# Heads of a hybrid layer: z units in the attention stage, gate units behind the heads, recurrence steps at every fifth matmul, half-height groups of two heads joined

## The chip, the cores and the metric

The kernel runs on one core of a Trainium2 chip. The metric is the device time of one execution in microseconds (us), as the median of several runs. TensorE (PE, its weight loads PEld) multiplies matrices into PSUM, ScalarE (ACT) and VectorE (DVE) empty PSUM and work on SBUF, GpSimd (POOL) and SyncE (SP) mainly issue transfers here.

## What is computed

One layer of a hybrid decoder trunk on x (1024 tokens x 1024 channels, f32). Its input is modulated by a conditioning vector c, projected by `w_in`, and goes through two mixers side by side, windowed attention and a gated delta rule; sigmoid gates merge them, and a squared-ReLU MLP follows.

```
mod = silu(c) @ w_ada + b_ada
sh1, sc1, gt1, sh2, sc2, gt2 = split(mod, 6)
u = x * (1 + sc1) + sh1
qa, ka, va, dq, dk, dv, z, b_raw, a_raw, g_a, g_b = split(u @ w_in)
y_a = sliding_window_attention(qa, ka, va, sinks) @ w_oa
y_b = gated_deltanet(dq, dk, dv, z, b_raw, a_raw, ...) @ w_ob
mixed = (sigmoid(g_a) * y_a + sigmoid(g_b) * y_b) @ w_out
x = layer_norm(ALPHA * x + (1 + gt1) * mixed)
u2 = x * (1 + sc2) + sh2
x = layer_norm(ALPHA * x + (1 + gt2) * (relu(u2 @ w_ff1 + b_ff1)**2 @ w_ff2 + b_ff2))
```

The gated delta net has 8 heads of width 128. q, k and v go through a causal convolution of four taps and a Silu. Then each head runs a recurrence over the tokens with a state of 128x128, and closes with a norm and a multiplication by silu(z):

```
v_new = u_c - w_c @ state
o_c = q_c @ state + intra_c @ v_new
state = state * last_c + k_c.T @ v_new
o = o * rsqrt(mean(o * o) + RMS_EPS) * norm_w * silu(z)
```

## The kernel before

**The stream of main matmuls.** A projection is made 128 output channels at a time. Such a unit is 48 main matmuls: two halves of 512 tokens, eight blocks of input channels, and for each of these three products of f32 numbers split in a high and a low part (`wh`, `wl` of the weights, `uh`, `ul` of the input). `stream_unit` issues them, all on L253 in this part of the kernel. One main matmul is a moving tile of 128x512 with 128x128 weights. A counter goes up with every main matmul, and all other work is hung on it: `at(i, f)` runs the function f ahead of the i-th main matmul, `after(n, f)` runs it n matmuls from now. This writes the order of the program: each engine works through its own instructions in the order in which the functions issued them, and semaphores do the rest.

**The stages.** k convolutions and v of the attention come first. Then 26 units make the attention stage (`units_b`): 2 of k, 8 of q and 16 gate units, behind which the softmax work of the attention is hidden. The gate units are g_a and g_b; `gate_done` copies both halves of a unit to SBUF and stores them to DRAM. From main matmul Q0 on, 24 units make the heads stage: q, v and z of head 0, of head 1, and so on. Then come `w_oa` (8 units, called ya here), `w_ob` (yb), the output projection and the MLP.

**The heads.** A head's work is small steps among the main matmuls:
- `hd_load` fetches what an earlier stage left in DRAM for the head (`kT`, `kd`, `E`, `Re`, `TT`, `T2o`, and `T1`, `L21`, which are 64 high).
- `conv_done` takes q's and v's projections out of PSUM: ScalarE copies each half to `pad` (L958) and, scaled, to `qT` or `vT` (L959), VectorE adds three taps (L962), ScalarE does a Silu (L967). One half after another, so that a unit's two halves stand 24 matmuls apart.
- `hd_z` (L1064) and `hd_x` (L1074) finish the inverse of a 128x128 triangular block by two groups of eight matmuls of 64x64 with 64-high operands, the half-height groups; ScalarE copies their PSUM tile to `Z` (L1065) and to `TT` (L1079, two copies).
- `hd_kq` (L1103) multiplies k and q in four pairs of blocks, VectorE makes `E` of it (L1107); `hd_qturn` (L1090) and `hd_vturn` (L1121) transpose q and v.
- The recurrence has 8 chunks of three steps. `hd_a`: one matmul kT x St (L1133), then VectorE makes `rhs` (L1135). `hd_b`: one matmul TT x rhs (L1143), then ScalarE makes `vn` (L1145). `hd_c`: the state's update (L1153; VectorE adds it to `St`, L1158) and the output, two matmuls into PSUM tile "c" (L1166), which ScalarE squares (`junk`, L1168) and VectorE copies (`o`, L1169). Chunk 0 has no kT x St, and its `rhs` is a slice of `vr`.
- `hd_norm` (L1174 to L1184) takes one Sqrt on ScalarE (`fs`, L1176) and scales `o`; `hd_out` transposes `o` and multiplies it by `sz`, which GpSimd stores to `og_d`. `sz` is silu(z), made by ScalarE right from z's PSUM tile (`sz_done`, L1206).

**Where the steps stand.** HOP = 6: a step stands at every sixth main matmul, so a chunk takes 18 and a head 144, which are just the three units of a head. Head h's recurrence starts at R = Q0 + 140 + 144h (28 later for head 7, whose recurrence lies in ya). The groups of `hd_z` and `hd_x` stand alone, at Q0 + 144h + 74 and + 86 (for heads past the first).

**PSUM tiles.** mains: "mm". Tag "a" (two buffers): the recurrence's products. Tag "c" (one): its output. Tag "b" (two buffers): kq, z, x, the transposes. A group that asks for a third "b" tile takes the place of the one that is emptied first, and waits for its readers.

**Between them.** `ada_load`, `ada_add` and `ada_part` (L995 to L1023) compute the last four sections of `mod`: VectorE sums 8 weight rows in an accumulator, and PE sums it over partitions, for f below 4 by one matmul of 128x512 (L1009), for the others by four pairs of 128x1 (L1018). ScalarE splits every unit's weights to `wh` (L220), VectorE makes `wl` (L221), both for a whole unit at once.

Of the kernel before, what the change touches and what calls it, by code (L numbers as in the profile page):

```python
# [34 lines left out]
def hybrid_layer_kernel(ctx: ExitStack, tc: tile.TileContext,  # L35
# [112 lines left out]
    wseq = [in_cols(w_in, C_DK + h * P) for h in range(8)]  # L148
    gates = [C_GA + f * P for f in range(KT)] + [C_GB + f * P for f in range(KT)]
    units_b, gi_, qi_, ki_ = [], 0, 0, 0  # L150
    for kind in "gkqgqggqggqkqggqggqggqgggg":
        if kind == "g":
            units_b.append((kind, gi_))
            gi_ += 1
        elif kind == "q":
            units_b.append((kind, qi_))
            qi_ += 1
        else:
            units_b.append((kind, ki_))
# [46 lines left out]
    def after(n, f, *args):  # L206
        at(count[0] + n, f, *args)
# [573 lines left out]
    def gate_done(i):  # L781
        t = gpool.tile([P, S], F32, tag="gate", name="gate")

        def done(half, pt):
            A.activation(out=t[:, halves[half]], in_=pt, func=AF.Copy)
            if half == 1:
                nc.sync.dma_start(out=(ga_d if i < KT else gb_d)[i % KT], in_=t)
        return done
# [197 lines left out]
    def ada_load(i, f, k):  # L986
        w, lo = ada["w"][i % 3], ada_cols_of(f)
        if k < KT:
            nc.sync.dma_start(out=w, in_=w_ada[k * P:(k + 1) * P, lo:lo + HALF])
            after(28, ada_add, w, k)  # L990
        else:
            nc.sync.dma_start(out=w[0:1, :], in_=b_ada[None, lo:lo + HALF])
        if k == KT - 1 + (f < 4):
            after(28 if f < 4 else 35, ada_part, f, w[0:1, :])

# [6 lines left out]

    def ada_part(f, b):
        acc = ada["acc"][:, 0, :]
        lo = ada_cols_of(f)
        half = f % 2
        t = psum("a", 2)
        if f < 4:
            T.matmul(t, lhsT=ones, rhs=acc, start=True, stop=True)  # L1009

            def put():
                V.scalar_tensor_tensor(out=b, in0=t[0:1, :], scalar=1.0, in1=b, op0=ALU.add, op1=ALU.add)
                nc.gpsimd.dma_start(out=gt_d[f // 2:f // 2 + 1, halves[half]], in_=b)
            after(5, put)
            return
        dst = (sh2 if f < 6 else sc2)[:, 4 * half:4 * half + 4]
# [13 lines left out]
    items = [(f, k) for f in range(KT) for k in range(KT + (f < 4))]  # L1030
    at(Q0 + 20, ada_open)
    for i, (f, k) in enumerate(items):
        at(Q0 + 170 + 13 * i, ada_load, i, f, k)

    def hd_load(h):
# [3 lines left out]
        T1 = d["T1"] = big4("T1", shape=[P, 4, 64])  # L1039
        L21 = d["L21"] = big4("L21", shape=[P, 4, 64])  # L1040
        T2o = d["T2o"] = big4("T2o", shape=[64, 4, 64])
# [10 lines left out]
        nc.gpsimd.dma_start(out=d["kd"], in_=kd_d[h])  # L1052
        d["ssq"] = pc.tile([P, NT], F32, tag="ssq", name="ssq")
        d["sso"] = pc.tile([P, NT], F32, tag="sso", name="sso")
        d["vr"], d["o"] = big4("vr"), big4("o")

# [90 lines left out]
    def hd_c(h, n):  # L1147
# [20 lines left out]
        after(4, lambda: A.activation(out=junk(), in_=op_[:, 0:P], func=AF.Square, accum_out=d["sso"][:, n:n + 1]))  # L1168
# [20 lines left out]
    def hd_out(h, half):  # L1189
        d = heads[h]  # L1190
        tp = psum("b", 2)
        for j in range(4):
            T.transpose(tp[:, chunk(j)], d["o"][:, chunk(4 * half + j)], ident)

# [6 lines left out]

    def sz_done(h):
        def done(half, pt):
            if half == 0:
                heads[h]["sz"] = big4("sz")
            A.activation(out=heads[h]["sz"][:, halves[half]], in_=pt, func=AF.Silu)  # L1206
        return done

    HOP = 6
    for h in range(8):  # L1210
        b = Q0 + 144 * h
        at(max(b, OPEN + 1), hd_load, h)
        late = max(b, OPEN + 1)
        for half in range(2):
            at(b + (56 if h else 68) + 24 * half, hd_qturn, h, half)
            at(max(b + 62, late + 40) + 24 * half, hd_kq, h, half)
            at(b + (98 if h else 104) + 24 * half, hd_vturn, h, half)
        at(max(b + 74, late + 50), hd_z, h)
        at(max(b + 86, late + 70), hd_x, h)
        R = b + (140 if h < 7 else 168)  # L1220
# [22 lines left out]

    for h in range(8):
        heads[h]["qT"] = pce.tile([P, S], F32, tag="qT", name="qT", bufs=2)
        stream_unit(uh, ul, conv_done(pce, h, heads[h]["qT"]))
        heads[h]["vT"] = pce.tile([P, S], F32, tag="vT", name="vT")
        stream_unit(uh, ul, conv_done(pce, 16 + h, heads[h]["vT"]))
        if h == 7:
            for k in range(KT):  # L1250
                at(count[0] + (0, 0, 0, 26, 36, 32, 38, 44)[k], attn_load, k)
                at(count[0] + (8, 14, 20, 38, 55, 50, 60, 66)[k], attn_split, k)
        stream_unit(uh, ul, sz_done(h), interleave=h == 7)

# [11 lines left out]

    CLOSE = R + 3 * HOP * NT + 36
    oh, ol = [None] * KT, [None] * KT
# [769 lines left out]
```

## Time and profile before

| what | value |
|---|---|
| median of 3 runs | 1820.82 us (1819.68 to 1826.78) |
| the profiled execution | 1820.36 us, of which its span is 1818.6 |
| mean granted TensorE clock | 0.995 |
| busy: DVE, ACT, POOL | 69%, 56%, 17% of the span |
| heads stage | about 548 to 890 us |
| ya stage, with head 7's recurrence | 890 to 975 us |

One execution was profiled. Times of day in it are us from the start of its span, and a line number is that of the kernel before unless the text says otherwise. A row of an engine's timeline has the start, the duration, the engine, the line, the operation, output <- inputs, weights and moving shape, the count; in brackets stands the idle time ahead of it and what ended it. A row of the windows has the stretch in us, its length, and for PE, its weight loads, DVE, ACT, POOL and SP the busy time and the count of instructions, then the granted clock, the DMA share and the GB/s.

### The profile page before, as it was taken

Reading aid. Unit: us, or ns where it says so; the run is one execution under the profiler, and the core shown is the slowest. Engines: PE = TensorE matmul, PEld = TensorE weight load, DVE = VectorE, ACT = ScalarE, POOL = GpSimd, SP = SyncE. Lnnn points to the kernel's source line nnn. Section 1 sums busy time; section 2 is a strip of 40 time slices with the busy share of each in tenths; the row PEclk is TensorE's granted clock in tenths of the full one; section 3 lists DMA queues with packets and bytes.
Section 4 is the critical chain, followed back from the end, with each engine's and each line's share of the span. In section 5 each row is a group of like instructions: output and inputs, shape, how many; then the busy total and the mean of one; then the engine's idle time right before and its main releaser. Section 6 shows DMA issues by size and latency. Waiting matters only on the chain.

```text
span 1818.6 us, 26129 instructions
## 1 busy us (share of the span) xinstructions
PE 1801.8 (99%) x9161; PEld 1512.8 (83%) x9161; DVE 1260.7 (69%) x2362; ACT 1017.5 (56%) x2304; POOL 304.2 (17%) x458
## 2 busy tenths in 40 slices
PE   8999999999999999999999999999999999999998
PEld 6988888888888888888888888888888888888887
DVE  6688688887854666666654445789777766576697
ACT  4699678888874555555554322466555554434341
POOL 0233234444331000000001100002222220000000
PEclk8999999999999999999999999999999999999999
DMA  9756722232257555554456543459887879755671
GB/s 275 209 199 204 231 68 89 66 104 80 78 194 173 153 147 157 152 154 137 135 176 235 165 149 139 138 157 315 292 295 265 286 281 390 258 185 186 199 264 47
DMA packets 262237, 337.73 MB, mean 186 GB/s; under 512 B 26213, under 2 KB 171318, under 8 KB 261850
## 3 DMA queue, kind: packets, MB, share of 16 engines
q1 hardware_dynamic: 223642, 216.09, 38.1%
q0 software_dynamic: 30320, 103.20, 17.0%
q10 hardware_dynamic: 8144, 16.78, 2.6%
q8 instruction: 72, 1.18, 0.3%
q14 instruction: 59, 0.48, 0.1%
HBM read 231.40 MB, written 102.51 MB: 184 GB/s over the span
## 4 chain that ended last, share of the span: by engine, by line
PE 90%; DVE 3%; ACT 2%; DMA 1%; issue 1%; POOL 0%; ACTq 0%; DVEq 0%; POOLq 0%; SPq 0%
PE mm L253 40%; PE mm L1899 8%; PE mm L1959 7%; PE a L1959 4%; PE b L1899 4%; PE b L1959 4%; PE a L1899 3%; PE c L1959 2%; PE c L883 2%; PE mm L1525 1%; PE mm L191 1%; PE mm L192 1%; PE mm L193 1%; PE a L809 1%; PE a L1525 1%; PE a L808 1%
## 5 line engine op out<-in xcount | busy, mean ns | idle before, releaser
L253 PE MATMUL mm<-uh,wl 128*128 128x512 f32 x800 | 330.1, 413 | 0.0
L253 PE MATMUL mm<-ul,wh 128*128 128x512 f32 x800 | 314.7, 393 | 0.0
L253 PE MATMUL mm<-uh,wh 128*128 128x512 f32 x800 | 313.9, 392 | 0.0
L221 DVE TENSOR_TENSOR sp<-sraw,sp 128x1024 fp32r<-128x1024 f32 x112 | 132.7, 1220 | 75.7 <-ACT sp L220 75.7
L220 ACT ACTIVATE sp<-sraw 128x1024 fp32r<-128x1024 f32 x112 | 112.6, 1054 | 121.4 <-PE b L1959 75.4
L253 PEld LDWEIGHTS mm<-ul,wh 128*128 128x128 f32 x800 | 150.2, 188 | 31.8
L253 PEld LDWEIGHTS mm<-uh,wl 128*128 128x128 f32 x800 | 150.8, 188 | 26.3 <-issue 1.0
L253 PEld LDWEIGHTS mm<-uh,wh 128*128 128x128 f32 x800 | 150.9, 189 | 25.4 <-issue 1.0
L1959 PE MATMUL mm<-sp 128*128 128x512 f32 x528 | 136.0, 389 | 0.0
L1959 PEld LDWEIGHTS mm<-sp 128*128 128x128 f32 x528 | 98.8, 188 | 20.3
L221 DVE TENSOR_TENSOR wl<-wr,wh 128x1024 fp32r<-128x1024 f32 x80 | 98.3, 1228 | 8.4 <-ACT wh L220 6.5
L220 ACT ACTIVATE wh<-wr 128x1024 fp32r<-128x1024 f32 x80 | 83.9, 1049 | 20.6 <-PE c L1525 12.3
L1959 PE MATMUL a<-sp 128*128 128x512 f32 x336 | 92.3, 389 | 0.0
L816 DVE CUSTOM_DVE_ANT_0 nscore<-a,amask,nsink 128x256 f32<-128x256 f32 (+1 forms) x128 | 54.5, 464 | 44.8 <-PE a L809 44.5
L1959 PE MATMUL b<-sp 128*128 128x512 f32 (+1 forms) x336 | 79.7, 374 | 0.0
L1959 PEld LDWEIGHTS a<-sp 128*128 128x128 f32 x336 | 63.1, 188 | 13.1
L1145 ACT ACTIVATE vn<-a,brk 128x128 f32<-128x128 f32 x64 | 23.5, 367 | 89.1 <-PE a L1143 89.0
L1959 PEld LDWEIGHTS b<-sp 128*128 128x128 f32 x336 | 60.3, 188 | 11.2
L827 POOL TENSOR_TENSOR sm<-sm 128x256 f32<-128x256 f32 x56 | 50.9, 909 | 104.9 <-ACT sm L823 76.6
L221 DVE TENSOR_TENSOR wl<-fraw,wh 128x1024 fp32r<-128x1024 f32 x43 | 52.5, 1221 | 19.6 <-ACT wh L220 19.5
L823 ACT ACTIVATE sm<-nscore,stat 128x257 f32<-128x257 f32 (+1 forms) x128 | 62.0, 488 | 2.7 <-DVE stat L816 2.4
L220 ACT ACTIVATE wh<-fraw 128x1024 fp32r<-128x1024 f32 x43 | 44.9, 1055 | 31.0 <-PE b L1899 25.0
(539 smaller groups left out, 4646.6 us busy)
## 6 DMA issues: line engine op xcount, KB each, us to landing
wr<-in_w_in_dram SPq DMA_DIRECT2D x60, 512.0 KB, 3.9
sraw<-hf_d SPq DMA_DIRECT2D x54, 512.0 KB, 4.3
adaw<-in_w_ada_dram SPq DMA_DIRECT2D x73, 256.0 KB, 4.7
fraw<-in_w_ff_dram SPq DMA_DIRECT2D x32, 512.0 KB, 5.3
sraw<-wt_d SPq DMA_DIRECT2D x32, 512.0 KB, 4.5
hf_d<-t ACTq DMA_DIRECT2D x48, 256.0 KB, 3.8
wt_d<-wx POOLq DMA_DIRECT2D x48, 256.0 KB, 3.6
sraw<-in_w_ff_dram SPq DMA_DIRECT2D x22, 512.0 KB, 5.5
```

What stands on the lines that cost most here:

```text
L191: T.matmul(t, lhsT=wh[:, k, :], rhs=xh[k][:, sl], start=k == 0, stop=False)
L220: A.activation(out=hi, in_=src, func=AF.Copy)
L221: after(lag, lambda: V.tensor_tensor(out=lo, in0=src, in1=hi.bitcast(F32), op=ALU.subtract))
L253: T.matmul(ts[half], lhsT=w[:, k, :], rhs=xx[k][:, sl], start=k == 0 and m == 0, stop=k == KT - 1 and m == 2)
L816: V.tensor_tensor_reduce(out=ns[:, i, 1:1 + W], in0=sc[:, i * 2 * P:i * 2 * P + W], in1=amask[:, mo:mo + W], scale=-1.0, scalar=nsink[:, 2 ...
L823: A.activation(out=sm[:, i, 0:1 + W], in_=ns[:, i, 0:1 + W], func=AF.Exp, scale=-1.0, bias=st[:, i:i + 1], accum_out=st[:, 2 + i:3 + i])
L827: G.tensor_tensor(out=sm[:, :, 1 + P:1 + 2 * P], in0=sm[:, :, 1:1 + P], in1=sm[:, :, 1 + P:1 + 2 * P], op=ALU.add)
L883: T.matmul(av[:, 0:256], lhsT=vt[:, b, :], rhs=p_[:, m, :], start=p_ is full and m == 0, stop=p_ is prods[-1][1] and m == 1)
L1145: after(1, lambda: A.activation(out=vn, in_=Wp[:, 0:P], func=AF.Copy, scale=brk[:, n, h:h + 1]))
L1525: T.matmul(pt, lhsT=m[k][:, tok], rhs=w[:, k % 2, :], start=k == 0 and w is wh and m is mh, stop=k == KT - 1 and m is ml)
L1899: T.matmul(pt, lhsT=a[:, kk, :], rhs=b[k], start=begin and k == 0 and x_ == 0, stop=k == 3 and x_ == 2, skip_group_check=True)
L1959: T.matmul(to, lhsT=a[:, f, t * P:(t + 1) * P], rhs=b[:, f, lo:up], start=(begin or own) and s % NS == 0 and f == 0 and x_ == 0, stop=s % ...
```

## The change

**Units.** The 16 gate units of the attention stage are now z of the 8 heads and g_a; `gate_done` stores z to a new DRAM tile `z_d`. The heads stage has q and v of each head, and the 8 units of g_b: g_b 0, 1 and 2 ahead of q of heads 2, 4 and 6, the other five behind v of head 7. `gb_done` copies each half of a g_b unit and stores it. The number of main matmuls is the same. `hd_gate` has GpSimd fetch z of a head to `sz`, and `hd_silu` has ScalarE take its Silu in SBUF, 40 and 45 matmuls later.

**Steps.** HOP = 5, PER = 120: head h's recurrence starts at R = Q0 + 144 + 120h, and all eight end within the heads stage. `hd_norm` stands 2 matmuls behind the place where the next head's chunk 0 starts, `hd_out` at 20 and 25 behind it.

**Half-height groups.** `hd_x` of head h and `hd_z` of head h+1 are at one place, R - 55, behind `hd_kq`'s second half (only z of head 0 stands alone). `T1` and `L21` have one buffer and are loaded a head ahead (`hd_solved`).

**Around it.** For f below 4 ada's sum over partitions takes the form that it had for the others; the rows of `b_ada` aren't loaded. qT has three buffers, `sz`, `T2o` and `o` one. The attention's output is loaded and split at other places in the last unit, and CLOSE, from which ya's pools open, is counted from the number of units.

```diff
-    gates = [C_GA + f * P for f in range(KT)] + [C_GB + f * P for f in range(KT)]
+    gates = [C_Z + f * P for f in range(8)] + [C_GA + f * P for f in range(KT)]
...
+    units_h = [("q", 0), ("v", 0)]
+    for h in range(1, 8):
+        units_h += [("g", h // 2 - 1)] * (h % 2 == 0) + [("q", h), ("v", h)]
+    units_h += [("g", i) for i in range(3, 8)]
...
-        if f < 4:
-            T.matmul(t, lhsT=ones, rhs=acc, start=True, stop=True)
...
+    def hd_gate(h):
+        heads[h]["sz"] = big4("sz", bufs=1)
+        nc.gpsimd.dma_start(out=heads[h]["sz"], in_=z_d[h])
+
+    def hd_silu(h, half):
+        o = heads[h]["sz"][:, halves[half]]
+        A.activation(out=o, in_=o, func=AF.Silu)
...
-    HOP = 6
+    HOP = 5
+    PER = 3 * HOP * NT
+    R0 = Q0 + 144
     for h in range(8):
...
+        R = R0 + PER * h
+        early = max(R - 118, OPEN + 1)
+        at(early, hd_load, h)
         for half in range(2):
...
+            at((R - 80 if h else R0 - 74) + 25 * half, hd_kq, h, half)
+            at((R - 85 if h else R0 - 70) + 25 * half, hd_qturn, h, half)
+            at(R - 40 + 20 * half, hd_vturn, h, half)
+            at(R + 75 + 5 * half, hd_silu, h, half)
+        if h == 0:
+            at(early + 50, hd_z, 0)
+        at(R - 55 if h else early + 70, hd_x, h)
+        if h < 7:
+            at(R - 55 if h else early + 70, hd_z, h + 1)
+        at(R + 35, hd_gate, h)
...
+        at(R + PER + 2, hd_norm, h)
+        at(R + PER + 20, hd_out, h, 0)
+        at(R + PER + 25, hd_out, h, 1)
```

**The change in the engines' order.** Three places; line numbers are those of each kernel. The first is ScalarE where a head ends and the next one starts its chunk 0: from the square of the last output (`junk`) to the next head's first `vn`. Before, between heads 0 and 1:

```order
L1168 ACTIVATE junk,sso<-c 128x128
L1176 ACT_TABLE_LOAD
L1176 ACTIVATE fs<-fs,eps_q 128x8
L1206 ACT_TABLE_LOAD
L1206 ACTIVATE sz<-mm 128x512
L1145 ACTIVATE vn<-a,brk 128x128
```

Now, between heads 1 and 2:

```order
L1178 ACTIVATE junk,sso<-c 128x128
L956 ACTIVATE pad<-mm 128x512
L957 ACTIVATE qT<-mm,convc 128x512
L1186 ACT_TABLE_LOAD
L1186 ACTIVATE fs<-fs,eps_q 128x8
L1155 ACTIVATE vn<-a,brk 128x128
```

Where z's half and a second table load stood, the two copies of a conv half now stand, ahead of the load. Between heads 0 and 1, and 4 and 5, a weight split (`wh`) stands there too, between `junk` and `pad`.

The second is TensorE at the half-height groups, with what each waits for; the number behind an engine's name is a semaphore's value at that place, left as printed. Before, z of a head between a recurrence step and a main matmul:

```order
L1143 MATMUL a<-rhs,TT_6181 128x128 [waits DVE_49]
L1064 MATMUL b<-T_6935,L_6936 64x64 [waits DMAHW7_49,DMAHW0_49,Activation_49]
L1064 MATMUL b<-T_6935,L_6936 64x64 [waits DMAHW3_49,DMAHW2_49]
L1064 MATMUL b<-T_6935,L_6936 64x64 x6
L253 MATMUL mm<-uh_125,wl 128x512
```

Now, the last of x of head 1 and z of head 2:

```order
L1084 MATMUL b<-TT_6181,Z 64x64
L1084 MATMUL b<-T2o,Z 64x64
L1074 MATMUL b<-T_6943,L_6944 64x64 [waits DMAHW0_49,DMAHW1_49,PE_49,Activation_49]
L1074 MATMUL b<-T_6943,L_6944 64x64 [waits DMAHW3_49]
L1074 MATMUL b<-T_6943,L_6944 64x64 x6
L251 MATMUL mm<-uh_131,wl 128x512
```

z has moved to right behind x (L1084), which stands behind kq's second half; its first matmul has a wait on PE and on ScalarE beside those on its loads.

The third is VectorE at the third chunk of a head, up to `rhs`, with the last `hd_out` multiplication (`sz`) of the head before. Before:

```order
L1196 SCALAR_TENSOR_TENSOR sz<-b,convc,sz 128x512
L956 MEMSET pad 128x3
L999 TENSOR_SCALAR ada<-ada,c_col 128x512
L1158 SCALAR_TENSOR_TENSOR St<-St,last,a 128x128
L221 TENSOR_TENSOR wl<-wr,wh 128x1024
L962 SCALAR_TENSOR_TENSOR qT<-pad,convc,qT 128x512
L1135 SCALAR_TENSOR_TENSOR rhs<-a,negegc,vr 128x128
```

Now, for head 2:

```order
L1168 SCALAR_TENSOR_TENSOR St<-St,last,a 128x128
L1206 SCALAR_TENSOR_TENSOR sz<-b,convc,sz 128x512
L219 TENSOR_TENSOR wl<-wr,wh 128x1024
L960 SCALAR_TENSOR_TENSOR vT<-pad,convc,vT 128x512
L1145 SCALAR_TENSOR_TENSOR rhs<-a,negegc,vr 128x128
```

`sz` has moved from ahead of the state's update to between it and the weight split.

More of the change, by code (lines that the diff above doesn't have):

```diff
@@ L77, in hybrid_layer_kernel @@
     e_d = dram.tile([8, P, S], F32, name="e_d")
+    z_d = dram.tile([8, P, S], F32, name="z_d")
     re_d = dram.tile([8, P, S], F32, name="re_d")
@@ L786, in done @@
             if half == 1:
-                nc.sync.dma_start(out=(ga_d if i < KT else gb_d)[i % KT], in_=t)
+                nc.sync.dma_start(out=(z_d if i < 8 else ga_d)[i % 8], in_=t)
         return done
@@ L980, in ada_open @@
         w2 = gpool.tile([P, 2, HALF], F32, tag="gate", name="adaw")
+        ada["col"] = gpool.tile([P, 4], F32, name="gcol", bufs=1)
         ada["w"] = [ada["acc"][:, 1, :], w2[:, 0, :], w2[:, 1, :]]
@@ L987, in ada_load @@
         w, lo = ada["w"][i % 3], ada_cols_of(f)
[L988 to L994, printed above, removed]
+        nc.sync.dma_start(out=w, in_=w_ada[k * P:(k + 1) * P, lo:lo + HALF])
+        after(28, ada_add, w, k)
+        if k == KT - 1:
+            after(35, ada_part, f)
     def ada_add(w, k):
@@ L1007, in ada_part @@
         t = psum("a", 2)
-        if f < 4:
-            T.matmul(t, lhsT=ones, rhs=acc, start=True, stop=True)
[L1011 to L1016, printed above, removed]
+        dst = ada["col"] if f < 4 else (sh2 if f < 6 else sc2)[:, 4 * half:4 * half + 4]
         for j in range(4):
@@ L1028, in ada_part @@
         after(4, put)
-    items = [(f, k) for f in range(KT) for k in range(KT + (f < 4))]
+    items = [(f, k) for f in range(KT) for k in range(KT)]
     at(Q0 + 20, ada_open)
@@ L1033, in hybrid_layer_kernel, with hd_solved @@
         at(Q0 + 170 + 13 * i, ada_load, i, f, k)
+    def hd_solved(h):
+        d = heads[h]
+        T1 = d["T1"] = big4("T1", shape=[P, 4, 64], bufs=1)
+        L21 = d["L21"] = big4("L21", shape=[P, 4, 64], bufs=1)
+        half = [slice(0, 64), slice(64, P)]
+        for i in range(2):
+            nc.sync.dma_start(out=L21[half[i]], in_=l21_d[h, :, i::2, :])
+            nc.sync.dma_start(out=T1[half[i]], in_=t_d[h, 0, i::2].rearrange("n a s -> a n s"))
     def hd_load(h):
@@ L1038, in hd_load @@
         TT = d["TT"] = TTs[h % 2]
[L1039 to L1041 removed]
+        T2o = d["T2o"] = big4("T2o", shape=[64, 4, 64], bufs=1)
         half = [slice(0, 64), slice(64, P)]
@@ L1052, in hd_load, with o_chunk @@
         nc.gpsimd.dma_start(out=d["kd"], in_=kd_d[h])
+        if h == 0:
+            hd_solved(0)
+        if h < 7:
+            hd_solved(h + 1)
         d["ssq"] = pc.tile([P, NT], F32, tag="ssq", name="ssq")
         d["sso"] = pc.tile([P, NT], F32, tag="sso", name="sso")
-        d["vr"], d["o"] = big4("vr"), big4("o")
+        d["vr"] = big4("vr")
+        d["o"] = [big4(f"o{i}", shape=[P, HALF], bufs=1) for i in range(2)]
+    def hd_gate(h):
[4 more added lines that the diff above has]
+        A.activation(out=o, in_=o, func=AF.Silu)
+    def o_chunk(d, n):
+        return d["o"][n // 4][:, chunk(n % 4)]
     def hd_z(h):
@@ L1192, in hd_out @@
         for j in range(4):
-            T.transpose(tp[:, chunk(j)], d["o"][:, chunk(4 * half + j)], ident)
+            T.transpose(tp[:, chunk(j)], o_chunk(d, 4 * half + j), ident)
         def put():
@@ L1200, in hd_out, with gb_done @@
         after(2, put)
[L1202 removed]
+    def gb_done(i):
+        ts = []
         def done(half, pt):
[L1204 to L1209 removed]
+            t = big4("gz", shape=[P, HALF])
+            A.activation(out=t, in_=pt, func=AF.Copy)
+            nc.sync.dma_start(out=gb_d[i, :, halves[half]], in_=t)
+        return done
+    HOP = 5
+    PER = 3 * HOP * NT
+    R0 = Q0 + 144
     for h in range(8):
[L1211 to L1213 removed]
+        R = R0 + PER * h
+        early = max(R - 118, OPEN + 1)
+        at(early, hd_load, h)
         for half in range(2):
[L1215 to L1220, printed above, removed]
+            at((R - 80 if h else R0 - 74) + 25 * half, hd_kq, h, half)
+            at((R - 85 if h else R0 - 70) + 25 * half, hd_qturn, h, half)
+            at(R - 40 + 20 * half, hd_vturn, h, half)
+            at(R + 75 + 5 * half, hd_silu, h, half)
+        if h == 0:
+            at(early + 50, hd_z, 0)
+        at(R - 55 if h else early + 70, hd_x, h)
+        if h < 7:
+            at(R - 55 if h else early + 70, hd_z, h + 1)
+        at(R + 35, hd_gate, h)
         for n in range(NT):
@@ L1242, in attn_split @@
             split_s(ah[k][:, halves[half]], al[k][:, halves[half]], araw[k][:, halves[half]], 3)
[L1244 to L1253, printed above, removed]
+    for kind, h in units_h:
+        if kind == "q":
+            heads[h]["qT"] = pce.tile([P, S], F32, tag="qT", name="qT", bufs=3)
+            stream_unit(uh, ul, conv_done(pce, h, heads[h]["qT"]))
+        elif kind == "v":
+            heads[h]["vT"] = pce.tile([P, S], F32, tag="vT", name="vT")
+            stream_unit(uh, ul, conv_done(pce, 16 + h, heads[h]["vT"]))
+        else:
+            if h == 7:
+                for k in range(KT):
+                    at(count[0] + (0, 0, 0, 0, 0, 32, 38, 44)[k], attn_load, k)
+                    at(count[0] + (8, 14, 20, 26, 32, 50, 56, 62)[k], attn_split, k)
+            stream_unit(uh, ul, gb_done(h), interleave=h == 7)
     def ya_done(f):
@@ L1265, in ya_done @@
         return done
-    CLOSE = R + 3 * HOP * NT + 36
+    CLOSE = Q0 + 48 * len(units_h) + 34
     oh, ol = [None] * KT, [None] * KT
```

36 lines of the change are left out of this document (12 added, 24 removed).

## The prediction

> **What bounds the kernel now.** I read the page first, then the windows of the two stages that the change touches, then PE's waits there, and last the timelines of PE, ScalarE and VectorE around the steps that move. The page gives the granted clock in 40 slices and the chain that ended last, by engine:
>
> ```profile
> PEclk8999999999999999999999999999999999999999
> PE 90%; DVE 3%; ACT 2%; DMA 1%; issue 1%; POOL 0%; ACTq 0%; DVEq 0%; POOLq 0%; SPq 0%
> ```
>
> The windows (PE, weight loads, DVE, ACT, POOL) of the heads stage and of ya:
>
> ```profile
> 548.00:890.00 342.00, 342.00 (x2058) 290.55 (x2057) 211.71 (x467) 178.22 (x519) 28.64 (x47) 1.00 0.55 153
> 890.00:975.00 85.00, 84.98 (x471) 71.66 (x471) 44.10 (x100) 44.28 (x104) 6.41 (x12) 1.00 0.44 144
> ```
>
> PE is busy for all of the 342.00 and all but .02 of the 85.00, at full clock. So there is next to nothing to win, except matmul time itself; the question is what the change makes PE wait for. Its waits on an engine in the two stages, as the weight loads show them:
>
> ```profile
> PEld a L1153 <- ACT vn L1145: 1.8, 6, 0.3
> PEld a L1133 <- DVE St L1161: 0.2, 1, 0.2
> ```
>
> Six waits for `vn` at a head's start. A weight load runs ahead of its matmul, so PE itself loses less; by the steps' starts I read about .1 for each, .6 in all. The change pulls the steps nearer together (five mains rather than six) and puts new work ahead of them, so I price each place where PE's path and the other engine's path are now near each other.
>
> **What a step costs PE.** A two-pass step among mains:
>
> ```profile
> 780.61 0.39 PE L253 MATMUL mm<-uh,wh 128*128 128x512 f32 x1
> 780.84 0.39 PE L253 MATMUL mm<-ul,wh 128*128 128x512 f32 x1
> 781.07 0.38 PE L1143 MATMUL a<-rhs,TT 128*128 128x128 f32 x2
> 781.21 0.48 PE L253 MATMUL mm<-uh,wl 128*128 128x512 f32 x1
> 781.53 0.40 PE L253 MATMUL mm<-uh,wh 128*128 128x512 f32 x1
> ```
>
> Mains start .23 apart. From 780.84 to 781.53 it is .69, so the step costs .69 - .46 = .23: .14 to the next main, and that main lasts .09 longer. The steps keep their number and this price whether five or six mains lie between; HOP alone changes no PE work.
>
> Now z, which stood alone, and x:
>
> ```profile
> 794.18 0.68 PE L1064 MATMUL b<-T,L 64*64 64x64 f32 x16
> 794.79 0.50 PE L253 MATMUL mm<-uh,wl 128*128 128x512 f32 x1
> 795.13 0.39 PE L253 MATMUL mm<-uh,wh 128*128 128x512 f32 x1
> ...
> 799.99 0.27 PE L1074 MATMUL b<-TT,Z 64*64 64x64 f32 x1
> ...
> 800.45 0.22 PE L1074 MATMUL b<-T2o,Z 64*64 64x64 f32 x1
> ...
> 800.72 0.77 ACT L1079 ACTIVATE TT<-b 64x256 f32<-64x256 f32 x2 [1.67 <-PE b L1074]
> ```
>
> z costs .61 + (.34 - .23) = .72. Its 8 pairs of passes take .46 (799.99 to 800.45, as x's do); the other .26 goes when z stands straight behind x. Seven joins: 7 x .26 = **-1.8**.
>
> But z needs a "b" tile while kq's and x's are both in use; the order shows z's first matmul with a wait on ScalarE behind x. x's copies start .73 behind x's first matmul (800.72) and last .77 for both: z can start at 1.50. Unhindered it would start at about .46 + .06 = .52. So PE stands for 1.50 - .52 = .98 at each of the six places of heads 1 to 6, and by the same rows about .8 at head 0's, where z waits on VectorE's four `E` products: 5.9 + .8 = **+6.7**. Here nothing covers it: PE's queue is in order, and all mains behind z wait with it. Bounds: 0, if kq's place is free first, and 1.3, if a Silu (.5) stands half done ahead of the copies.
>
> **A head's start (chunk 0).** Before, the last output of a head, the norm, z's Silu and `vn`:
>
> ```profile
> 670.28 1.28 ACT L1176 ACT_TABLE_LOAD   x1
> 671.57 0.30 ACT L1176 ACTIVATE fs<-fs,eps_q 128x8 f32<-128x8 f32 x1
> 671.89 1.28 ACT L1206 ACT_TABLE_LOAD   x1
> 673.19 0.60 ACT L1206 ACTIVATE sz<-mm 128x512 f32<-128x512 f32 x1
> 673.68 0.36 ACT L1145 ACTIVATE vn<-a,brk 128x128 f32<-128x128 f32 x1
> 674.09 0.49 PE L1153 MATMUL a<-vn,kd 128*128 128x128 f32 x2
> ```
>
> The table load keeps ScalarE for 1.29, Sqrt .32, and `vn` lets PE go .41 behind its start. This is the row against me: two loads and a Silu stood ahead of `vn` here, and PE lost about .1. It is so near because 12 mains lay between c and c; now 10 do, and the two conv copies come in their place. How long those take and how late they start:
>
> ```profile
> 637.27 0.39 PE L1166 MATMUL c<-vn,E 128*128 128x128 f32 x2
> 637.75 0.28 ACT L1168 ACTIVATE junk<-c 128x128 f32<-128x128 f32 x1 [1.17 <-PE c L1166]
> 638.19 0.40 PE L253 MATMUL mm<-uh,wl 128*128 128x512 f32 x1
> 638.62 0.60 ACT L958 ACTIVATE pad<-mm 128x512 f32<-128x512 f32 x1 [0.50 <-PE mm L253]
> 639.11 0.68 ACT L959 ACTIVATE qT<-mm,convc 128x512 f32<-128x512 f32 x1
> ...
> 643.47 0.28 ACT L1168 ACTIVATE junk<-c 128x128 f32<-128x128 f32 x1
> 643.74 1.05 ACT L220 ACTIVATE wh<-wr 128x1024 fp32r<-128x1024 f32 x1
> ```
>
> R is a multiple of 24 behind Q0, so each head's start meets the end of a half. *Even heads 2, 4, 6:* from the half's last main, ScalarE: .43 to `pad`, .49, .68, load 1.29, Sqrt .32, `vn` .41 = 3.62. PE in the same time: 11 mains and a b step to c, 11 x .23 + .23 = 2.76. PE waits .86, three times 2.6. *Odd heads 1 and 5:* a weight split (1.05, less the overlap of .10 that the ends of other copies show) stands ahead of `pad`: from the last output .48 + .27 + .95 + .49 + .68 + 1.29 + .32 + .41 = 4.89, against PE's .14 + .09 + 15 x .23 + .23 = 3.91: .98, twice 2.0. Head 3 about .1 (ada's eight small products fall on PE there), head 7 about .4 (one copy). Sum **+5.1**. What reaches it from below is `vn` sent ahead of the load, which the order does not show; from above, a drain around the load (rival D).
>
> The Trainium skill, "ScalarE: Activation LUTs", section "What ACT_TABLE_LOAD costs", gives 1.28 us for the load and about 1.38 us more of drain for each switch. The load agrees with the row; Sqrt starting at 671.57 leaves no room for the drain, so by the trace it isn't charged here.
>
> **Chunks with VectorE in the way.** From the state's update to `rhs`:
>
> ```profile
> 636.82 0.38 PE L1153 MATMUL a<-vn,kd 128*128 128x128 f32 x2
> 637.24 0.35 DVE L1158 SCALAR_TENSOR_TENSOR St<-St,last,a 128x128 f32<-128x128 f32 x1 [0.69 <-PE a L1153]
> ...
> 631.96 0.35 DVE L1158 SCALAR_TENSOR_TENSOR St<-St,last,a 128x128 f32<-128x128 f32 x1 [0.68 <-PE a L1153]
> 632.22 1.22 DVE L221 TENSOR_TENSOR wl<-wr,wh 128x1024 fp32r<-128x1024 f32 x1
> 633.36 0.75 DVE L962 SCALAR_TENSOR_TENSOR qT<-pad,convc,qT 128x512 f32<-128x512 f32 x1
> 634.02 0.35 DVE L1135 SCALAR_TENSOR_TENSOR rhs<-a,negegc,vr 128x128 f32<-128x128 f32 x1
> ```
>
> Third chunk of heads 2, 4, 6, where `sz` now stands behind `St`: .42 + .26 + .66 (`sz`, as the tap) + 1.14 + .66 + .35 + .05 = 3.54. PE from c's first matmul to the b step: .45 + .14 + .09 to the second main, 10 mains 2.30, the a step .23 = 3.21. Wait .33 each, 1.0, and one more .66 for an ada sum at head 4: **+1.7**. Last chunk of heads 1 and 5, with two ada sums and no `sz`: .42 + .26 + 1.14 + 3 x .66 + .35 + .05 = 4.20 against 3.21 + four transposes at .11 = 3.65: .55 each, **+1.1**. Other places (head 7's `hd_out` behind attention splits .7, its Silu's load .4, chunk 1 of two heads .1 each): **+1.3**, estimates by the same pitches.
>
> **The rest.** The g_b copies take the place of z's Silus, one for one; ada's 128x512 product for four columns is eight small passes four times, within .2. `sz` goes over DRAM and its second table load now stands at R + 75. Its way:
>
> ```profile
> og_d<-sz POOLq DMA_DIRECT2D x8, 512.0 KB, 3.9
> ga<-ga_d POOLq DMA_DIRECT2D x8, 512.0 KB, 4.0
> E<-e_d SPq DMA_DIRECT2D x7, 512.0 KB, 7.4
> ```
>
> `sz` has one buffer: the fetch (`hd_gate`, R + 35) waits on GpSimd's queue for the old `sz`'s store, which `hd_out` lets go at about R + 27. Store and fetch take 3.9 + 4.0 = 7.9 us, 11.3 if the fetch is as slow as `E`'s loads; to the Silu at R + 75 there are 48 mains and about 9 steps, 48 x .23 + 9 x .3 = 13.7. So it has room, and behind it on GpSimd's queue stand only the next heads' loads, which are wanted a head later.
>
> **Sum.** Waits 6.7 + 5.1 + 1.7 + 1.1 + 1.3 = 15.9, less 1.8 for the joins and .6 for the old waits: +13.5. From the profiled run's own 1820.36, of which 1818.6 is span: **1833.9 us**. That run lies .46 under the median, less than the runs scatter (1819.68 to 1826.78), so I add nothing.
>
> **Rivals.**
> - *A, one of the two large terms is hidden.* For: each stands on one row's latency. Without z's wait 1833.9 - 6.7 = 1827.2; without the waits of heads' starts and chunks (5.1 + 1.7 + 1.1) 1826.0. Chance .23.
> - *B, the other side: no wait binds.* z gets kq's place, whose `E` products are done when x ends, and `vn` passes as it did at 673.68, with .1 lost. Price: -1.8 - .6 and about 1 for the rest: 1819. It decides if ScalarE's chain at a start stays under PE's 2.76, that is if the copies come .9 earlier. Against: copies can't begin before the half's last main has ended. Chance .08.
> - *C, `sz` comes late.* If store and fetch take 15.7 us rather than 7.9, ScalarE stands at the Silu with `vn` queued behind it, and PE with it: 2 us for each of 7 heads, 1833.9 + 14 = 1848. For: one buffer and a store ahead of the load; against: even 3.9 + 7.4 fits. Chance .10.
> - *D, a switch of tables costs more beside copies.* ScalarE idle for another 1.4 between its copies and the load at seven starts: 7 x 1.4 = 9.8 more, 1843.7. Against: 671.57. Chance .03. It is the rule of the Trainium skill's page above.
>
> **How the numbers follow.** The forecast holds .56. About .5% (9.1 us) is what a measurement can tell from no change. Slower by over that is above 1829.9: nearly all of the forecast (.50 of its .56, its terms being sums of small differences), C and D, and a little of A: .66. The rest of A, B and the forecast's low end: .32 the same; .02 faster, since nothing on the page leaves 9 us to win. The range reaches from A's lower values to D's: 1823 to 1845.
>
> **What would show it.** The waits after should list z (L1074) behind ScalarE's `TT` six times at about 1.0, the c step (L1163) behind `vn` (L1155) at about .9 at heads 1, 2, 4, 5, 6, and the b step (L1153) behind `rhs` at .3 to 1.0. ya should be free of waits. If PE's windows stay full, B holds; if ScalarE's Silu of `sz` waits on a DMA, C. I am wrong if z starts within .2 of x's end.

## The result, and the profile after

The changed kernel takes 1837.04 us (median of 4 runs, 1835.71 to 1841.01), the kernel before 1820.66: a ratio of 1.0086, 95% interval 1.0059 to 1.0113, so 16.4 us slower. 1833.9 was forecast. The profiled execution after is the one of 1835.71, with a span of 1833.9.

The clock and the chain that ended last on the page after:

```profile
PEclk8999999999999999999999999999999999999999
PE 89%; DVE 3%; ACT 3%; DMA 1%; issue 1%; POOL 0%; ACTq 0%; SPq 0%; DVEq 0%; POOLq 0%
```

The clock is the same; PE has lost a point of the chain, ScalarE gained one. The starts of the mains show a slip of the prediction: main Q0 starts at 537.25 us before and Q0 + 1152 at 916.05, so the heads stage is that stretch, and the cuts at 548 and 890 ran through it. The sum doesn't rest on them. Before, cut at the mains Q0 and Q0 + 1152 (PE, weight loads, DVE, ACT, POOL):

```profile
537.25:916.05 378.80, 378.80 (x2276) 321.82 (x2274) 232.64 (x512) 199.38 (x575) 32.00 (x52) 1.00 0.55 155
```

After, from Q0 to Q0 + 1152, and on to Q0 + 1392, where before has head 7 done as well:

```profile
536.43:942.52 406.09, 391.62 (x2390) 333.02 (x2388) 242.96 (x558) 219.81 (x630) 38.05 (x62) 1.00 0.58 166
942.52:996.92 54.40, 54.40 (x242) 45.05 (x240) 25.18 (x36) 25.89 (x37) 6.37 (x12) 1.00 0.78 263
```

In the heads stage PE now idles for 406.09 - 391.62 = 14.5 us; it idled not at all before. The following stretch, which has no head's work left in it, is free of idle time and shorter. Q0 to Q0 + 1392 takes 460.5 us against 444.3 before: **+16.2**. Ahead of Q0 the two differ by .8, behind it by .0: all of the loss lies here. The waits of PE itself from Q0 on, after:

```profile
PE b L1074 <- ACT TT L1089: 4.3, 5, 0.9
PE a L1163 <- ACT vn L1155: 3.3, 6, 0.6
PE b L1074 <- DMA T<-t_d: 3.0, 1, 3.0
PE a L1153 <- DVE rhs L1145: 2.0, 5, 0.8
PE b L1203 <- ACT o L1192: 0.9, 1, 0.9
PE b L1074 <- DMA adaw<-in_w_ada_dram: 0.9, 1, 0.9
```

Before, this list is empty. The last line is z's sixth join, put down to a transfer that z doesn't use: the weight loads' list has all six behind `TT`:

```profile
PEld b L1074 <- ACT TT L1089: 6.0, 6, 1.0
```

Four of the places, as the timelines after show them. First the join of x of head 1 and z of head 2:

```profile
600.16 1.06 PE L1113 MATMUL b<-qT,kT 128*128 128x128 f32 x8
601.15 0.27 PE L1084 MATMUL b<-TT,Z 64*64 64x64 f32 x1
...
601.88 0.77 ACT L1089 ACTIVATE TT<-b 64x256 f32<-64x256 f32 x2 [0.92 <-PE b L1084]
602.70 0.75 PE L1074 MATMUL b<-T,L 64*64 64x64 f32 x16 [0.87 <-ACT TT L1089]
```

z starts 1.55 behind x's first matmul and .05 behind the end of ScalarE's two copies. Next chunk 0 of head 1, where a weight split stands ahead of the conv copies on ScalarE:

```profile
620.20 1.05 ACT L218 ACTIVATE wh<-wr 128x1024 fp32r<-128x1024 f32 x1
621.14 0.59 ACT L956 ACTIVATE pad<-mm 128x512 f32<-128x512 f32 x1
621.62 0.69 ACT L957 ACTIVATE qT<-mm,convc 128x512 f32<-128x512 f32 x1
622.33 1.28 ACT L1186 ACT_TABLE_LOAD   x1
623.62 0.30 ACT L1186 ACTIVATE fs<-fs,eps_q 128x8 f32<-128x8 f32 x1
623.83 0.35 ACT L1155 ACTIVATE vn<-a,brk 128x128 f32<-128x128 f32 x1
624.23 0.49 PE L1163 MATMUL a<-vn,kd 128*128 128x128 f32 x2 [0.63 <-ACT vn L1155]
```

ScalarE has no gap from the split to `vn`. And the third chunk of head 4 on VectorE, from the state's update to `rhs`, the worst of its kind:

```profile
765.10 0.35 DVE L1168 SCALAR_TENSOR_TENSOR St<-St,last,a 128x128 f32<-128x128 f32 x1 [1.08 <-PE a L1163]
765.36 0.75 DVE L1206 SCALAR_TENSOR_TENSOR sz<-b,convc,sz 128x512 f32<-128x512 f32 x1
766.02 0.74 DVE L997 SCALAR_TENSOR_TENSOR ada<-adaw,c_col,ada 128x512 f32<-128x512 f32 x1
766.68 1.22 DVE L219 TENSOR_TENSOR wl<-wr,wh 128x1024 fp32r<-128x1024 f32 x1
767.81 0.74 DVE L960 SCALAR_TENSOR_TENSOR vT<-pad,convc,vT 128x512 f32<-128x512 f32 x1
768.48 0.34 DVE L1145 SCALAR_TENSOR_TENSOR rhs<-a,negegc,vr 128x128 f32<-128x128 f32 x1
```

Last the first join (x of head 0, z of head 1), for which the forecast had a small price:

```profile
561.91 0.27 PE L1084 MATMUL b<-TT,Z 64*64 64x64 f32 x1
...
565.54 1.00 PE L1074 MATMUL b<-T,L 64*64 64x64 f32 x16 [2.95 <-DMA T<-t_d]
```

z of head 1 waits for its `T`, and not for VectorE's `E`.

### The profile page after: what moved, and what is told of

The parts are those of the page before. It is cut to its first block, busy times and chain, and to the rows that moved or that the text cites. A ratio compares the mean times of both kernels' runs of the same rounds, so it can differ in the third digit from the quotient of the medians.

```text
span 1833.9 us, 26304 instructions
## 1 busy us (share of the span) xinstructions
PE 1800.4 (98%) x9184; PEld 1512.9 (82%) x9185; DVE 1258.2 (69%) x2366; ACT 1024.8 (56%) x2320; POOL 309.9 (17%) x466
## 4 chain that ended last, share of the span: by engine, by line
PE 89%; DVE 3%; ACT 3%; DMA 1%; issue 1%; POOL 0%; ACTq 0%; SPq 0%; DVEq 0%; POOLq 0%
PE mm L251 38%; PE mm L1919 8%; PE mm L1979 7%; PE a L1979 4%; PE b L1919 4%; PE b L1979 4%; PE a L1919 3%; PE c L1979 2%; PE mm L1545 2%; PE c L881 2%; PE a L1545 1%; PE mm L189 1%; PE mm L191 1%; PE mm L190 1%; PE a L807 1%; PE a L806 1%
## 5 line engine op out<-in xcount | busy, mean ns | idle before, releaser
L251 PE MATMUL mm<-uh,wl 128*128 128x512 f32 x800 | 319.9, 400 | 0.0
L251 PE MATMUL mm<-ul,wh 128*128 128x512 f32 x800 | 319.7, 400 | 0.0
L251 PE MATMUL mm<-uh,wh 128*128 128x512 f32 x800 | 319.0, 399 | 0.0
L866 POOL TENSOR_SCALAR_AFFINE_SELECT pl<-ph 128x512 fp32r<-128x512 f32 x56 | 53.7, 959 | 41.8 <-DVE ph L859 38.1
```

Of the source, the lines that this page charges most:

```text
L251: T.matmul(ts[half], lhsT=w[:, k, :], rhs=xx[k][:, sl], start=k == 0 and m == 0, stop=k == KT - 1 and m == 2)
L866: G.affine_select(out=flat4(part), in_=flat4(full), pattern=[[0, 4], [1 if odd else -1, P]], compare_op=ALU.is_ge if odd else ALU.is_gt, f ...
```

## The experiments

Below, a **place** is all that PE does between two mains; its price is the distance from the main ahead to the second main behind, less two pitches of .227, as the prediction priced the two-pass step. **Extra time** is the stretch from Q0 to Q0 + 1392 of the profiled execution, less 1392 pitches: 128.8 us before, 144.9 after (+16.2). Each experiment was profiled once, so a place's price is that of one execution, and the totals are medians of several. Medians of before, run beside the experiments, were 1820.9 to 1821.0.

**1. z's PSUM tile.** z's group takes tag "c", which is free there; order and work stay.

```diff
-        zp = psum("b", 2)
+        zp = psum("c", 1)
```

> Edit: z's group gets the PSUM tile of tag "c", so it no longer needs the place that x holds; order, places and work stay. Theory (PE stands behind ScalarE's TT copies): the six joined rows fall from 3.5 us to about 1.93 + 0.5 = 2.45, the waits on TT (6.0) vanish, the total is 1837.0 - 6.3 = 1830.7. Rival (the 64-high groups themselves cost more when one follows the other): the rows stay at 3.5 and the total at 1837. The first join keeps its 4.9 in both, if a late load of T is its cause.

Measured: 1832.36 us, ratio to before 1.0065 (1.0049 to 1.0080). All six joined places fell from 3.48 to 3.55 to 2.39; the same place without z (x of head 7, still there) costs 1.93, so z behind x is .46, its passes and nothing else. z now starts ahead of x's copies:

```profile
604.07 0.63 PE L1074 MATMUL c<-T,L 64*64 64x64 f32 x16
604.29 0.77 ACT L1089 ACTIVATE TT<-b 64x256 f32<-64x256 f32 x2 [0.91 <-PE b L1084]
```

The theory holds: the price was the PSUM place, 1.09 to 1.16 at each of six joins, 6.8 in all, not the form of the matmuls. The total is 1.7 above the expectation. In the profiled execution the first join, left alone here, cost 6.95 (4.86 after), and with this longer wait PE's granted clock went to half (the 0.50 in the row below) for 6.83 us, of which the place's price holds only a part:

```profile
564.06:570.89 6.83, 5.10 (x27) 4.25 (x28) 1.19 (x2) 1.53 (x9) 0.20 (x1) 0.50 0.27 68
```

The mains there stand .43 apart rather than .23, and up to Q0 + 102 the two together cost 3.5 more than after. A further .8 is one chunk of head 2; its cause wasn't followed.

**2. Two buffers for `T1` and `L21`.**

```diff
-        T1 = d["T1"] = big4("T1", shape=[P, 4, 64], bufs=1)
-        L21 = d["L21"] = big4("L21", shape=[P, 4, 64], bufs=1)
+        T1 = d["T1"] = big4("T1", shape=[P, 4, 64])
+        L21 = d["L21"] = big4("L21", shape=[P, 4, 64])
```

> Edit: T1 and L21 get two buffers again, so that head 1's are fetched with head 0's and not after z of head 0. Theory (one buffer delays the fetch): the first join falls from 4.86 us to 1.3, or to 2.1 if it then waits for VectorE's E; the total is 1837.0 - 3 = 1834. Rival (the queues at the stage's start are full, the fetch is late with any buffer): the wait on T stays at 2 to 3 us, 1837.

Measured: 1834.64 us, 1.0074 (1.0059 to 1.0089). The first join fell from 4.86 to 2.02, and now it waits for VectorE:

```profile
562.28 1.13 DVE L1117 SCALAR_TENSOR_TENSOR E<-b,rk,E 128x128 f32<-128x128 f32 x4 [1.77 <-PE b L1113]
563.46 0.75 PE L1074 MATMUL b<-T,L 64*64 64x64 f32 x16 [0.37 <-DVE E L1117]
```

So one buffer delayed the fetch: it could be issued only behind z of head 0, 20 mains ahead of its use. The wait on `E` that was forecast (.8) is there, half as long, once the fetch is out of the way.

**3. The norm behind the first `vn`.**

```diff
-        at(R + PER + 2, hd_norm, h)
-        at(R + PER + 20, hd_out, h, 0)
-        at(R + PER + 25, hd_out, h, 1)
+        at(R + PER + 7, hd_norm, h)
+        at(R + PER + 23, hd_out, h, 0)
+        at(R + PER + 28, hd_out, h, 1)
...
-        d["o"] = [big4(f"o{i}", shape=[P, HALF], bufs=1) for i in range(2)]
+        d["o"] = [big4(f"o{i}", shape=[P, HALF], bufs=2 - i) for i in range(2)]
```

> Edit: the norm stands at R + PER + 7 rather than + 2, behind the next head's first vn, with hd_out at + 23 and + 28 and a second buffer for the first half of o. Theory (table load, Sqrt and the two conv copies together are longer than PE's 2.76): the c step of chunk 0 at heads 1, 2, 4, 5, 6 falls from 1.31-1.35 us to about 0.5, 4.2 in all; the third chunk of heads 2, 4, 6 may lose up to 0.4 more each, since sz comes ahead of the state. Total 1833 to 1834. Rival (the copies alone are too late, or the weight split): the rows stay above 1.0, total 1836 to 1837.

Measured: 1833.11 us, 1.0063 (1.0046 to 1.0079). The c step of chunk 0 costs .45 at all eight heads; 4.7 us are gone. Chunk 0 of head 1 there:

```profile
625.28 0.59 ACT L956 ACTIVATE pad<-mm 128x512 f32<-128x512 f32 x1
625.76 0.69 ACT L957 ACTIVATE qT<-mm,convc 128x512 f32<-128x512 f32 x1
626.67 0.37 ACT L1155 ACTIVATE vn<-a,brk 128x128 f32<-128x128 f32 x1 [0.22 <-PE a L1153]
627.06 1.28 ACT L1186 ACT_TABLE_LOAD   x1
627.57 0.38 PE L1163 MATMUL a<-vn,kd 128*128 128x128 f32 x2
```

The copies alone leave ScalarE idle ahead of `vn`; with load and Sqrt they don't. The third chunks, expected to lose a little, gained 1.1 in sum (1.34 rather than 1.77 at head 4), as `sz` now comes partly ahead of the state's update. The total came down by 3.9 and not by 5.8: the first join was long again (6.68) and the granted clock was 0.50 for 6.82 us with it, 3.2 more than after together in the profiled execution.

**4. Without most of ada's sums.**

```diff
     def ada_add(w, k):
         acc = ada["acc"][:, 0, :]
+        if k:
+            return
```

> Leaves out seven of the eight terms of each of ada's sums on VectorE (the loads and PE's small products stay). Theory (in the third and last chunks the sums stand between the state's update and rhs): head 4's third chunk falls from 1.77 us to 1.1, the last chunks of heads 1 and 5 from 0.91 to 0.25, the third chunks of heads 2 and 6 stay at 1.1 (sz); total 1837.0 - 2.0 = 1835. Rival (another instruction makes rhs late there, the sums only fill gaps): the rows stay, 1837.

Measured: 1840.54 us, 1.0108 (1.0093 to 1.0123), so the total missed. The places themselves went as expected: head 4's third chunk from 1.77 to 1.11, the last chunks of heads 1 and 5 from .91 to .37, and 1.11 at heads 2, 4 and 6, where `sz` stays. From Q0 + 102 on the extra time falls by the 2.0 expected. But the first join took 12.43 us, 7.6 more than after, and the clock was 0.50 for 10.24 us with it:

```profile
PE b L1076 <- DMA T<-t_d: 9.7, 2, 8.9
551.77 15.88 SPq L987 DMA_DIRECT2D adaw<-in_w_ada_dram  x4
568.33 0.60 SPq L1034 DMA_DIRECT2D T<-t_d  x1
```

The edit did this itself. With most of the sums gone, four loads of `adaw` stand ahead of the fetch of `T` in SyncE's queue. Two of them wait for earlier loads of `adaw` to land, and `T` goes out behind them at 568.33 rather than at 556.99. All four executions took 1839.71 us or more, so it is no chance of the profiled one. The total therefore says nothing on the sums; the places do.

**5. HOP = 5 alone, in the kernel before.**

```diff
-    HOP = 6
+    HOP = 5
```

> Edit: the kernel before with HOP = 5 alone, so that a head's recurrence takes 120 mains of its 144 and a pause follows. Theory (the spacing costs nothing by itself, only what then stands ahead of a step): the steps keep their 0.23 and 0.68, the waits for vn at the heads' starts go (about 1.0 in the trace of before), total 1819 to 1822. Rival (steps at every fifth main are too near each other): about 0.1 more for each of 64 x 2 steps, total 1830 or more.

Measured: 1828.98 us, 1.0049 (1.0031 to 1.0067): slower, against the expectation, though not as the rival has it. The steps keep their prices (.23, .68), chunk 0's too (.45 to .46). PE's waits show what came instead:

```profile
PE b L1193 <- ACT o L1182: 2.3, 5, 0.6
PE mm L253 <- ACT sz L1206: 2.3, 1, 2.3
```

`hd_out` comes 16 mains behind the norm, when ScalarE still has the table load, a weight split, z's Silu with its load, and the copies of v's transposes to do before it can scale `o`. The second wait is at the start of ya, where z's last Silu now meets the attention's splits.

**6. The same, with `hd_out` ten mains later for heads 0 to 5.**

```diff
-        at(late + (25 if h == 6 else 19 if h == 7 else 16), hd_out, h, 0)
-        at(late + (36 if h == 6 else 24 if h == 7 else 22), hd_out, h, 1)
+        at(late + (25 if h == 6 else 19 if h == 7 else 26), hd_out, h, 0)
+        at(late + (36 if h == 6 else 24 if h == 7 else 32), hd_out, h, 1)
```

> Edit: the kernel before with HOP = 5 as in the earlier run, and hd_out ten mains later for heads 0 to 5. Theory (what made HOP = 5 slower there is hd_out, which waits for ScalarE's scaled o, and not the spacing of the steps): the waits of 3.9 us at hd_out go, total 1829.0 - 3.9 = 1825; the wait of 2.5 where ya starts and the rows that no longer share a place stay. Rival (the spacing): 1829.

Measured: 1824.02 us, 1.0014 (1.0006 to 1.0023). The waits at `hd_out` are gone; against before 2.1 us of extra time remain, and the wait at ya's start alone is 2.3. So the spacing itself costs nothing that could be seen.

**7. The change with HOP = 6.** PER is 144, the g_b units stand behind each head's v, and the attention's loads and CLOSE are placed for a last head in ya.

```diff
-    HOP = 5
+    HOP = 6
...
+    for h in range(8):
+        units_h += [("q", h), ("v", h), ("g", h)]
```

> Edit: the changed kernel with HOP = 6 (PER = 144), g_b's units one behind each head, the attention's loads as before, head 7's recurrence in ya again; joins, z over DRAM and one buffer for T1 stay. Theory: joined rows stay at 3.5 and the first join at 5 to 7; chunk 0 has 13 mains, 3.2 against 3.62, so its c step falls from 1.31 to 0.9 but at all seven heads; waits for rhs nearly go (3.67 against 3.54 and 4.2). Total 1829 to 1832. Rival (the spacing makes all the loss): 1821. Rival (the join makes all of it): 1837.

Measured: 1837.43 us, 1.0087 (1.0069 to 1.0105), above the expectation. Joined places cost 3.46 with z and 1.85 without, each with most of the step that follows one main later: z's 1.61 is that of the change (3.55 less 1.93). Chunk 0's c step costs .46 at heads 1 to 6, and not .9: at a head's start it is a g_b half that ends, with one copy and not two, so ScalarE's 3.62 was 2.94 against PE's 3.2. I had overlooked that. What filled the total were the first join (4.65, with the clock at 0.50 for 3.41 us) and new waits at head 7 among the attention's splits, where ya costs 5.6 more than before:

```profile
PE a L1142 <- DVE St L1167: 1.6, 2, 1.2
PE mm L250 <- ACT ah L217: 1.6, 1, 1.6
```

So neither rival holds: spacing is not all of the loss, and not the join alone either; each arrangement has its own collisions.

**8. All heads 12 mains later.**

```diff
-    R0 = Q0 + 144
+    R0 = Q0 + 156
```

> Edit: R0 = Q0 + 156, twelve mains later, so that no half ends where a head starts. Theory (what counts is all that stands with the table load ahead of vn): now the conv's Silu stands there with a second table load: from the last output 0.48 + 0.39 + 1.29 + 0.32 + 1.28 + 0.54 + 0.41 = 4.71 against PE's 3.91, so chunk 0's c step is about 1.25 at all seven heads; total 1837 to 1840. Rival (only the two conv copies at a half's end matter): the rows fall to 0.5, total 1833.

Measured: 1835.75 us, 1.0084 (1.0068 to 1.0100). The rival falls: with no conv copies at a head's start, the c steps of chunk 0 still cost 1.28 to 1.48 at heads 1, 3, 4, 5 and 6; heads 2 and 7 are at .45, which the theory had at 1.25 as well. At head 2 eight small products of ada fall between the two outputs and make PE's path .8 longer; at head 7 no conv Silu stands there, and ScalarE waits .90 for PE. ScalarE ahead of head 1's `vn`:

```profile
620.67 1.28 ACT L1186 ACT_TABLE_LOAD   x1
622.16 0.30 ACT L1186 ACTIVATE fs<-fs,eps_q 128x8 f32<-128x8 f32 x1 [0.21 <-DVE fs L1185]
622.48 1.28 ACT L965 ACT_TABLE_LOAD   x1
623.78 0.63 ACT L965 ACTIVATE qT<-qT 128x512 f32<-128x512 f32 x1
624.31 0.35 ACT L1155 ACTIVATE vn<-a,brk 128x128 f32<-128x128 f32 x1
```

What counts is the sum of what stands ahead of `vn` with the load, whichever instructions these are, against PE's path beside it. The total stayed below the 1837 to 1840 expected: two heads didn't wait, and the first join was short this time (2.40).

**9. Four edits together:** 1, 2, 3, and head 7's `hd_out` 13 mains later.

```diff
+        at(R + PER + (23 if h < 7 else 36), hd_out, h, 0)
+        at(R + PER + (28 if h < 7 else 41), hd_out, h, 1)
```

> Edit: z in tag "c", two buffers for T1 and L21, the later norm, and head 7's hd_out 13 mains later, all in the changed kernel. Theory (the terms are separate and add up): 6.7 + 2.9 + 4.7 + 1.1 + 1.3 come off the 16.1 of the heads stage, total 1820 to 1822, no different from before. Rival (waits taken away come back at the next place): 1826 or more.

Measured: 1819.97 us, .9996 (.9986 to 1.0005). The extra time is 127.4, 17.6 below the change. The edits one by one gave 6.8 + 2.8 + 4.7 + 1.1 = 15.4 at their places. This run itself adds .6 at the first join, where both causes are gone, and 1.4 at head 7: 17.4. The terms add up. What PE still waits for from Q0 on:

```profile
PE a L1153 <- DVE rhs L1145: 1.2, 3, 0.4
PE a L1163 <- ACT vn L1155: 0.2, 1, 0.2
```

**10. Two more edits on top:** ada's loads 6 mains later, and head 7's Silu of `sz` 4 mains earlier.

```diff
-        at(Q0 + 170 + 13 * i, ada_load, i, f, k)
+        at(Q0 + 176 + 13 * i, ada_load, i, f, k)
...
-            at(R + 75 + 5 * half, hd_silu, h, half)
+            at(R + (75 if h < 7 else 71) + 5 * half, hd_silu, h, half)
```

> Edit: the four edits together, and two more: ada's loads start 6 mains later, so that its sums leave the stretches between the state's update and rhs, and head 7's Silu of sz stands 4 mains earlier, ahead of a b step rather than of a c step. Theory: 2.1 (rhs at heads 1, 4, 5 and 6) and 0.5 (head 7) come off 1820.0, total 1817.4. Rival (the sums' grid of 13 mains meets other chunks): no change against the four edits, 1820.

Measured: 1818.51 us, .9992 (.9983 to 1.0000); extra time 127.6, no less than without them. The rival holds: the last chunks of heads 1 and 5 fell from .91 to .37 and head 4's third from 1.31 to .80, but those of heads 2 and 6 went from .66 and .80 to 1.29 and 1.33, another chunk from .67 to 1.16, and head 3's last chunk lost .7. The grid of 13 mains beside chunks of 15 met other chunks in the new position; only these two positions were tried. The interval reaches 1.0000, so this isn't shown to beat the kernel before.

**11. The join alone, in the kernel before:** z of head h+1 behind x of head h, z in tag "c", `T1` and `L21` loaded a head ahead with their two buffers.

```diff
-        at(max(b + 74, late + 50), hd_z, h)
-        at(max(b + 86, late + 70), hd_x, h)
+        if h == 0:
+            at(late + 50, hd_z, 0)
+        at(b + 93 if h else late + 70, hd_x, h)
+        if h < 7:
+            at(b + 93 if h else late + 70, hd_z, h + 1)
```

> Edit: the kernel before with the join alone: z of head h+1 right behind x of head h, at Q0 + 144h + 93, z in tag "c", T1 and L21 loaded a head ahead with their two buffers. Theory (a half-height group costs 0.34 beside its passes, saved when it stands behind another): seven times 0.3 and no new wait, total 1820.9 - 2.2 = 1818.7. Rival (x and z away from kq and from a step cost more than the join saves, or z waits for o's copy in "c"): 1821 to 1823.

Measured: 1821.03 us, 1.0000 (.9991 to 1.0008). Six of seven joined places cost 1.28 beside the step that stands one main ahead, against 1.61 for the two groups apart (.81 and .80), but the first took 2.76 with a wait on `T`. Extra time 127.6 against 128.8: the profiled stretch shows 1.2 of the 2.2, the median none. A saving of this size is below what these runs tell apart.

## Why the prediction was right, point by point

Prices in us, from the starts of PE's instructions; "after" is the difference to before at the same places.

| term | forecast | after |
|---|---|---|
| joins of heads 1 to 6 (z's wait less what the join saves) | 5.9 - 1.6 = 4.3 | 4.7 |
| the first join | .8 - .3 = .5 | 3.2 |
| chunk 0, less the old waits | 5.1 - .6 = 4.5 | 3.7 |
| third chunk, heads 2, 4, 6 | 1.7 | 2.0 |
| last chunk, heads 1 and 5 | 1.1 | 1.4 |
| head 7's `hd_out` and Silu, chunk 1 of two heads | 1.3 | 2.1 |
| sum | 13.5 | 17.1 (the stretch: 16.2) |

The .9 between the places' sum and the stretch lies at other places, where the change groups steps, transposes and ada's products differently; it wasn't followed further.

**The likeliest case was the right one.** All large terms lie where the prediction put them: six waits of z at "about 1.0" (weight loads: 6.0 in six), the c step at heads 1, 2, 4, 5 and 6 late by .86 to .90 (1.31 to 1.35 less .45; forecast .86 and .98), and `rhs` late by .43 to 1.10 at the chunks named of heads 1, 2, 4, 5 and 6. Experiments 1, 3, 4 and 9 took each away by what it was said to rest on. The measured loss (16.4) passes the forecast one (13.5) by 2.9; the first join alone is 2.7 above its term. The part that follows the heads is free of waits, as the prediction said of ya.

**The step that failed** is the first join, priced "by the same rows about .8 at head 0's, where z waits on VectorE's four `E` products". It cost 4.86 us, where experiment 9 has 1.38: 3.5 of waiting, because `T` of head 1 came late. The prediction weighed one buffer for `sz` and traced its way through the queues, but not one buffer for `T1` and `L21`, which the change made at the same time: the fetch waits for z of head 0 and then has 20 mains and a "b" group, some 6 us, beside the other loads of heads 0 and 1. Experiment 2 shows both the cause and that the `E` products would have been next (.4).

**Mis-sized in small, and partly cancelling by luck:** the six waits of z came to 6.8 (1.09 to 1.16 each), not 5.9, but the joins saved 2.1, not 1.6, since z alone costs .81 beside a step (1.04 less .23) and not .72, so that their net is off by .4 alone. The third chunks waited .43 and .44 (1.10 at head 4) rather than .33 (.99), the last ones .68 rather than .55. Chunk 0 was .08 too dear at each of heads 1 and 5, and the old waits that go there were 1.0 by the prices of the places before (.46 without a wait), not .6; head 7's `hd_out` was put at .7 and measured 1.36, for ScalarE works splits of the attention's output in between its scalings of `o`.

**The rivals.** A and B fall with the table. C falls: no line of PE's or ScalarE's waits in the heads stage names `sz`'s fetch; store and fetch took 4.5 and 4.1 us (medians after). D falls as well: at 622.33 the load starts .02 behind the end of the copy, and Sqrt 1.29 later, so in this trace a switch beside conv copies costs the load and no more. The Trainium skill's page "ScalarE: Activation LUTs", section "What ACT_TABLE_LOAD costs", has the 1.28 of the load right; its further 1.38 of drain shows in none of these rows, nor in those of experiment 8, where two loads stand 1.81 apart with a Sqrt, and a wait of .21, between them.

## What to carry to other kernels

When groups are moved together to save an in-order engine their fixed cost, count the PSUM places that they hold at once: here the joins save some 2 us and one missing place costs 6.8. A buffer taken away is a dependency added: follow the load back to what frees its buffer, above all at the start of a stage, where many loads are under way. And an engine of 56% busy time still sets the end where its short queue ahead of one small instruction is longer than the path beside it; add up that queue, instruction by instruction, from rows of the same engine.

## What the runs showed that was not expected

The same place, a fetch of `T` into one buffer at the start of the heads stage, cost 4.86 us after, 4.65 in experiment 7, and 6.95 and 6.68 in experiments 1 and 3, whose edits don't touch it; the 12.43 of experiment 4 came from its own edit. After, one landing of a 64 KB transfer of short rows took from 2.2 to 8.4 us:

```profile
L1032 SPq DMA_DIRECT2D T<-t_d x16: 573/606/1590, 545.4 to 785.4; - x16
DMA to landing us min/median/max: 2.2/2.4/8.4
```

The slow one falls into a stretch in which the DMA engines are busy throughout (DMA share 1.08 from 550 to 565, and .33 in the ten us behind it):

```profile
550.00:565.00 15.00, 12.59 (x92) 10.27 (x90) 9.27 (x18) 7.12 (x20) 1.76 (x3) 1.00 1.08 331
```

A transfer's median says little of the one that is waited for. And a wait can cost more than itself: with this one the granted clock was half for 3.41 to 10.24 us in experiments 1, 3, 4 and 7, and full in the kernel after. The wait's length alone doesn't tell which it will be: PE stood 2.7 us on `T` in experiment 7, which had the half clock, and 3.0 in the kernel after, which had not.
